# Six steps of the third modulation vector in front of the fifth SSD tile's gate projection

## The chip, the cores and the metric

One core of a Trainium2 chip runs the whole kernel in one launch. The time is the device time of that core in microseconds (us). The engines are TensorE (PE, with its weight loads as PEld), VectorE (DVE), ScalarE (ACT), GpSimd (POOL) and SyncE (SP), which here only issues loads.

## The reference, cut to what matters

Two blocks of a sequence model on 512 tokens of width 1024. The change lies in the first block, in its SSD branch and its modulation vectors:

```python
mod = jax.nn.silu(c) @ w_mod[l] + b_mod[l]              # 1024 -> 6 x 1024
sh1, sc1, gt1, sh2, sc2, gt2 = jnp.split(mod[:, None, :], N_MOD, axis=-1)
...
p_lat = h_lat @ w_in                                    # latent tokens, 512
p_ctx = h_ctx @ w_in                                    # context tokens, 256
xs_l, bm_l, cm_l, dt_l, la_l = ssd_prepare(p_lat[..., XBC0:DT0], ...)
y_l, _, _ = ssd_bidir(xs_l, bm_l, cm_l, dt_l, la_l, hf_c, hb_c, True)
ssd_lat = ssd_output(y_l, xs_l, p_lat[..., Z0:XBC0], d_skip, ssd_g)   # gated by silu(z)
...
x = x + gt1 * o_lat
x = x + gt2 * conv_ffn(modulate(x, norm2_g[l], sh2, sc2), ...)
```

`sh1` and `sc1` (vectors 0 and 1) are needed before the projections. `gt1` (vector 2) and `sh2` (vector 3) are needed after the branches, long after the SSD part.

## The kernel before, in words

**Tiles.** The SSD branch has 2048 channels, worked on as 16 tiles of 128 channels (two heads each), in four groups of four tiles. `ssd_in(kt)` does the input side of tile `kt`: at the first tile of a group the group's B and C projections (`ssd_group`), then the tile's own `xs` projection (`both`: latent and context tokens, into PSUM tiles `pl` and `pc`), convolution, transposes, chunk states (`st`), and last the gate projection z (`proj(T_Z + kt, False)`, into `pl` alone) with its silu (`zs`). `ssd_heads(kt)` does the output side: decay rows loaded by POOL (`es`, `cf`), scans and products on VectorE, and the product `y` on TensorE (line 659, raised in priority). The loop runs `ssd_in(kt + 1)` and then `ssd_heads(kt)`, and after every fourth tile `ssd_out`, the output projection of a group (`po`). In this text B1, C1 are the projections of the second group, and xs4, z4 those of `kt` = 4, the fifth tile.

**A projection.** `dense` loads a weight block of 128 x 1024 by `load_w`: one load of 512 KB on SP's queue into a tile `raw` (three of them, tag "raw"), then ScalarE makes `whi` (line 183) and VectorE `wlo` (line 186), two tiles of each. `mm3` (lines 223 to 225) issues three matmuls for each of the 8 blocks of 128 inputs: 24 matmuls into `pl`, and for `both` 24 into `pc` as well. The results lie in four PSUM banks (`bank`, tag "d") until a convolution (lines 183 and 189: `cv` for `pl`, `cvc` for `pc`) or a silu has read them.

**Modulation steps.** `mod_steps(r, ...)` computes vector `r` in 8 steps. Each step loads one block of `w_mod` (512 KB, line 341, SP's queue, the same three `raw` tiles) and issues four matmuls of 32 columns that lie beside each other in the array (line 322, `mod`, eight records of the trace a step), into a PSUM tile of its own, tag "m". After the eighth step ScalarE copies the result (`modsb`), TensorE transposes it (`modt`) and VectorE adds the bias. Vectors 0 and 1 are done before the projections, vectors 2 and 3 in the SSD loop: the list `mods` has 16 steps, and the loop takes two after each of the tiles 5 to 12.

**Order.** The program's order is not the engines' order. A planner in the compiler simulates the engines and gives each the ready instruction of highest priority; earlier in the program is higher. `tc.issue_after(ins)` puts the instructions of its block behind `ins` on the engine that `ins` runs on, and adds no wait between engines. A `raw` tile is given back when its last reader is done: `wlo` for a weight, the matmuls of the step for a modulation block.

Of the kernel before, what the change touches and what calls it, by code (L numbers as in the profile page):

```python
# [21 lines left out]
KD = 8  # L22
# [19 lines left out]
T_XBC, T_DT, T_Q, T_K, T_Z, T_G = 0, 24, 25, 33, 35, 51  # L42
# [114 lines left out]
def emit(ctx, tc, A, out):  # L157
# [22 lines left out]
    V, S, G, T, DMA, QS = nc.vector, nc.scalar, nc.gpsimd, nc.tensor, nc.sync, nc.gpsimd  # L180

    def act(o, i, f, **kw):
        return S.activation(o, i, f, **kw)  # L183

    def tt(o, a, b, op, eng=V):
        return eng.tensor_tensor(o, a, b, op=op)  # L186

    def stt(o, a, s, b, op0, op1):
        return V.scalar_tensor_tensor(o, a, s, b, op0=op0, op1=op1)  # L189
# [9 lines left out]
    def col(n, i=0, w=1):  # L199
        o = COL_OFF[n][0] + i  # L200
        return cols[:, o:o + w]
# [9 lines left out]
    def bank(name="d"):  # L211
        return banks["p"].tile([P, 512], F32, tag="d", name=name, bufs=banks["n"])
# [14 lines left out]
    def dense(src, kts, acts, outs, k0=0, kall=None):  # L227

        kall = kall or kts
        done = 0  # L230
        while done < kts:
            n = min(8, kts - done)
            hi, lo = load_w(src[:, done * P:(done + n) * P], n * P)
            for j in range(n):
                k = k0 + done + j
                for (ah, al), ps in zip(acts, outs):
                    mm3(ps, hi[:, j * P:(j + 1) * P], lo[:, j * P:(j + 1) * P],
                        ah(k), al(k), k == 0, k == kall - 1)
            done += n

    def flat(ap):
        return ap.rearrange("p k m -> p (k m)")
# [65 lines left out]
    csil = cst.tile([P, 8, 32], F32, name="csil")  # L308
# [3 lines left out]
    act(csil[:, :, 0:2], cc, AF.Silu)  # L312

    mod_end = {}

    def mod_steps(r, src, step=2, bank=bank):

        ps = bank("mod")
        for k in range(KD):
            raw = src(k)  # L320
            for j in range(4):
                T.matmul(ps[32 * j:32 * j + 32, 0:256], lhsT=csil[:, k, :], rhs=raw[:, j * 256:(j + 1) * 256],
                         start=(k == 0), stop=(k == KD - 1))
            if k % step == step - 1 and k < KD - 1:
                yield
        sb = cst.tile([P, 256], F32, tag="modsb", name="modsb")
        mod_end[r] = act(sb, ps[:, 0:256], AF.Copy).ins
        pt = bank("modt")
        for b in range(2):
            T.transpose(pt[:, b * P:(b + 1) * P], sb[:, b * P:(b + 1) * P], ident)  # L330
        v = pt[:, 0:256].rearrange("p (b j r) -> p b j r", b=2, j=4)
        bm = col("bmod", r * 8, 8).rearrange("p (j b) -> p b j", b=2)
        tt(modx[:, r, :].rearrange("p (j b) -> p b j", b=2), v[:, :, :, 0], bm, ADD)
        if r < 2:
            tt(modc[:, r, :].rearrange("p (j b) -> p b j", b=2), v[:, :, :, 1], bm, ADD)
        yield

    def mod_raw(r):
        def src(k):
            raw = wp.tile([P, 1024], F32, tag="raw", name="raw", bufs=3)  # L340
            DMA.dma_start(out=raw, in_=A["w_mod"][k * P:(k + 1) * P, r * 1024:(r + 1) * 1024])
            return raw
        return src
# [10 lines left out]
    with pool("pin") as pin, tc.tile_pool(name="pn", bufs=1, space=PSUM, reuse_waits="tile") as pn:  # L354
# [24 lines left out]
        def pnm(name):  # L379
            return pn.tile([P, 512], F32, tag="m", name=name, bufs=1)  # L380

        run(mod_steps(1, mod_pair(1), 2, pnm))
        wdt = pin.tile([P, 1024], F32, name="wdt")
        wdh = pin.tile([P, 1024], F32R, name="wdh")
# [48 lines left out]
    def proj(t, both):  # L433
        a = bank("pl")
        if both:
            c = bank("pc")
            dense(flat(A["w_ta"][t]), KD, [actl, actc], [a, c[:, 0:LC]])
            return a, c[:, 0:LC]
        dense(flat(A["w_ta"][t]), KD, [actl], [a])
        return a  # L440
# [8 lines left out]
    ps = pss.enter_context(tc.tile_pool(name="pss", bufs=1, space=PSUM, reuse_waits="tile"))  # L449

    def pst(name="t"):
        return ps.tile([P, 512], F32, tag="t", name=name, bufs=2)
# [19 lines left out]
    def silu(o, v):  # L472
        with ExitStack() as st:
            for h in hold:
                st.enter_context(tc.issue_after(h))
            act(o, v, AF.Silu)
# [74 lines left out]
    def both(t, tag, bufs, tm, tmbufs):  # L551

        a, c = proj(t, True)
        xc = sp.tile([P, LC], F32, tag="xc", name="xc")
        x = sp.tile([P, L], F32, tag=tag, name=tag, bufs=bufs)
        convs(t, [(c, LC, xc), (a, L, x)])
        xt_ = sp.tile([P, 6, P], F32, tag=tm, name=tm, bufs=tmbufs)
        to_tm([(0, [xc[:, j * P:(j + 1) * P] for j in range(2)]),
               (2, [x[:, j * P:(j + 1) * P] for j in range(4)])], xt_)
        return x, xt_  # L560
# [3 lines left out]
    def ssd_group(g):  # L564
        bl, btm = both(16 + g, "bl", 1, "btm", 2)
        t = 20 + g
        a = proj(t, False)
        cl = sp.tile([P, L], F32, tag="cl", name="cl", bufs=2)
        convs(t, [(a, L, cl)])
        cbt = sp.tile([P, L], F32, tag="cbt", name="cbt", bufs=2)  # L570
        pt = pst("cb")
        for c in range(4):
            T.matmul(pt[:, c * P:(c + 1) * P], lhsT=bl[:, c * P:(c + 1) * P], rhs=cl[:, c * P:(c + 1) * P],
                     start=True, stop=True)
        act(cbt, pt, AF.Copy)
        grp[g] = (btm, cl, cbt)
# [4 lines left out]
    def ssd_in(kt):  # L581

        g = kt // 4
        if kt % 4 == 0:
            ssd_group(g)
        btm = grp[g][0]
        xs, xtm = both(kt, "xs", 3, "xtm", 2)
        hin = []
        for d in range(2):
            xw = sp.tile([P, 6, P], F32, tag="xw", name="xw", bufs=2)  # L590
            w0 = 64 + d * 32 + 2 * kt
            for c0, c1 in ((0, 5),) if d == 0 else ((0, 2), (3, 6)):
                tt(xw[:, c0:c1].rearrange("p c (h e) -> p c h e", h=2),
                   xtm[:, c0:c1].rearrange("p c (h e) -> p c h e", h=2),
                   dwt[:, c0:c1, w0:w0 + 2].unsqueeze(3).to_broadcast([P, c1 - c0, 2, 64]), MUL,
                   eng=V)
            pst_ = pst("st")
            for n in range(4):
                cs = (0, 1) if n == 0 else (ORDER[d][n - 1],)
                for x, c in enumerate(cs):  # L600
                    T.matmul(pst_[:, n * P:(n + 1) * P], lhsT=btm[:, c], rhs=xw[:, c],
                             start=(x == 0), stop=(x == len(cs) - 1))
            hst = sp.tile([P, 4, P], F32, tag="hst", name="hst", bufs=4)
            dec = tdec[:, d * 32 + 2 * kt:d * 32 + 2 * kt + 2]
            act(hst[:, 0], pst_[:, 0:P], AF.Copy)
            for n in range(1, 4):
                for j in range(2):
                    e_ = slice(64 * j, 64 * j + 64)
                    stt(hst[:, n, e_], hst[:, n - 1, e_], dec[:, j, n:n + 1], pst_[:, n * P + 64 * j:n * P + 64 * j + 64],
                        MUL, ADD)  # L610
            hin.append(hst)
        a = proj(T_Z + kt, False)
        zs = sp.tile([P, L], F32, tag="zs", name="zs", bufs=2)
        silu(zs, a)
        pend[kt] = (xs, xtm, hin, zs)
# [73 lines left out]
    def psm(name):  # L689
        return ps.tile([P, 512], F32, tag="m", name=name, bufs=1)  # L690

    mods = [st_ for r in (2, 3) for st_ in [mod_steps(r, mod_raw(r), 1, psm)] * 8]
    with tc.issue_after(loaded.ins), tc.issue_after(mod_end[0]):
        ssd_in(0)
    hold.clear()
    early.clear()
    for kt in range(16):
        if kt < 14:
            ssd_in(kt + 1)
        ssd_heads(kt)  # L700
        if kt >= 5 and kt < 13:
            for _ in range(2):
                next(mods.pop(0))
        if kt % 4 == 1 and kt > 1:
            if kt == 13:
                ssd_in(15)
            ssd_out(kt // 4 - 1)
# [11 lines left out]
    ps = psa.enter_context(tc.tile_pool(name="psa", bufs=1, space=PSUM, reuse_waits="tile"))  # L719
# [20 lines left out]
    for i in range(2):  # L740
        a, c = proj(T_K + i, True)
# [641 lines left out]
    for kc in range(4):  # L1383
        w_h, w_l = load_w(A["w_mv"][:, 2 * kc:2 * kc + 2].rearrange("p k m -> p (k m)"))
        for k2 in range(2):
            k = 2 * kc + k2
# [17 lines left out]
    def proj2(t):  # L1404
        a = bank("p2")
        dense(flat(A["w_tb"][t]), KD, [acth], [a])
        return a
# [13 lines left out]
    ps = sta.enter_context(tc.tile_pool(name="psf", bufs=1, space=PSUM, reuse_waits="tile"))  # L1421
# [11 lines left out]
    for q in range(6):  # L1433
        a = proj2(U_U + q)
# [344 lines left out]
    for kc in range(4):  # L1779
        raw = wp.tile([P, 1024], F32, tag="raw", name="raw", bufs=3)  # L1780
# [49 lines left out]
```

## Time and profile before

| | us |
|---|---|
| median of 3 runs (2028.99 to 2034.67) | 2029.27 |
| the profiled execution | 2029.36 |
| its span, first to last instruction | 2027.6 |
| TensorE busy | 1958.2 (97%) |
| VectorE busy | 1344.9 (66%) |
| ScalarE busy | 967.5 (48%) |

The rows further down are of this profiled execution. Times in them count from the start of the span. A row of the timeline begins with the start and the length in us; a bracket at its end is the idle time of the engine before it and what ended that. TensorE's matmuls overlap, so that the spacing of their starts, not the length of one, is what a matmul costs. The granted clock (PEclk) is 1.00 at 2.4 GHz and 0.50 at 1.2 GHz.

### The profile page before, as it was taken

The numbers are of one execution on the slowest core, as the hardware profiler recorded it, in microseconds if no ns is written. First come the engines' busy times: TensorE is split into PE (matmuls) and PEld (weight loads), VectorE is DVE, ScalarE is ACT, GpSimd is POOL, SyncE is SP. The second block draws the span as 40 slices with busy tenths as digits, with TensorE's granted clock in tenths as the row PEclk, the third lists the DMA queues.
The fourth block names the chain that finished last, engine by engine and source line by source line (L and its number), as shares of the span: only waits on it lengthen the run. The fifth ranks groups of instructions, "written<-read, shape, count | busy, mean of one in ns | idle before, by whom it ended". The sixth has DMA issues, their size and how long they took to land.

```text
span 2027.6 us, 29457 instructions
## 1 busy us (share of the span) xinstructions
PE 1958.2 (97%) x11312; PEld 1612.4 (80%) x11312; DVE 1344.9 (66%) x2375; ACT 967.5 (48%) x1825; POOL 214.2 (11%) x354
## 2 busy tenths in 40 slices
PE   6998999999999899999999999999999899999998
PEld 4787888888888777778777878878988677888887
DVE  6878877879567766457988885573587655524344
ACT  6745555454246665335433244554465644423233
POOL 2111111102020000001001210000532100000000
PEclk9998999999999999999999999999999999999999
DMA  7443545545322022343354643345764121333332
GB/s 297 116 146 125 158 140 178 182 129 170 94 63 63 22 84 88 100 125 110 116 169 128 218 145 97 105 123 167 193 178 130 47 66 58 135 96 88 104 97 90
DMA packets 84667, 250.48 MB, mean 124 GB/s; under 512 B 11632, under 2 KB 23280, under 8 KB 83760
## 3 DMA queue, kind: packets, MB, share of 16 engines
q1 hardware_dynamic: 67376, 199.45, 31.9%
q0 software_dynamic: 17152, 49.17, 7.8%
q8 instruction: 89, 1.46, 0.3%
q14 instruction: 50, 0.41, 0.1%
HBM read 228.78 MB, written 16.65 MB: 121 GB/s over the span
## 4 chain that ended last, share of the span: by engine, by line
PE 89%; DVE 5%; ACT 3%; DMA 1%; issue 1%; POOL 1%; SPq 0%; DVEq 0%; ACTq 0%; POOLq 0%
PE p L223 6%; PE p L225 6%; PE p L224 6%; PE pl L223 5%; PE pl L225 5%; PE pl L224 5%; PE po L223 3%; PE po L224 3%; PE po L225 3%; PE y L659 2%; PE pT L807 2%; PE ub L225 2%; PE pdn L225 2%; PE ua L225 2%; PE pdn L223 2%; PE ub L223 2%
## 5 line engine op out<-in xcount | busy, mean ns | idle before, releaser
L186 DVE TENSOR_TENSOR wlo<-raw,whi 128x1024 fp32r<-128x1024 f32 (+3 forms) x283 | 329.1, 1164 | 275.0 <-ACT whi L183 268.6
L183 ACT ACTIVATE whi<-raw 128x1024 fp32r<-128x1024 f32 (+3 forms) x283 | 282.8, 1001 | 445.3 <-PE p L224 135.0
L223 PE MATMUL pl<-hl,whi 128*128 128x512 f32 x528 | 212.5, 403 | 10.7 <-DVE cvc L189 8.2
L225 PE MATMUL pl<-hl,wlo 128*128 128x512 f32 x528 | 210.6, 399 | 1.0 <-DVE wlo L186 1.0
L224 PE MATMUL pl<-hl,whi 128*128 128x512 f32 x528 | 210.4, 398 | 0.0
L223 PE MATMUL p<-h,whi 128*128 128x512 f32 x504 | 200.2, 399 | 1.9 <-ACT uf L183 0.8
L225 PE MATMUL p<-h,wlo 128*128 128x512 f32 x504 | 199.7, 397 | 1.1 <-DVE wlo L186 1.1
L224 PE MATMUL p<-h,whi 128*128 128x512 f32 x504 | 199.6, 396 | 0.0
L223 PEld LDWEIGHTS pl<-hl,whi 128*128 128x128 f32 x528 | 100.8, 191 | 29.0 <-issue 10.4
L225 PEld LDWEIGHTS pl<-hl,wlo 128*128 128x128 f32 x528 | 100.6, 190 | 23.6 <-DVE wlo L186 1.7
L183 ACT ACTIVATE p<-s,nm 128x512 f32<-128x512 f32 (+4 forms) x128 | 80.1, 627 | 74.0 <-PE pT L807 34.2
L223 PEld LDWEIGHTS p<-h,whi 128*128 128x128 f32 x504 | 95.3, 189 | 22.9 <-ACT uf L183 1.2
L225 PEld LDWEIGHTS p<-h,wlo 128*128 128x128 f32 x504 | 95.1, 189 | 22.2 <-DVE wlo L186 2.0
L782 DVE TENSOR_REDUCE nm<-s 128x1 f32<-128x512 f32 (+4 forms) x128 | 76.6, 610 | 53.9 <-PE s L1592 28.7
L224 PEld LDWEIGHTS pl<-hl,whi 128*128 128x128 f32 x528 | 100.7, 191 | 13.8
L224 PEld LDWEIGHTS p<-h,whi 128*128 128x128 f32 x504 | 95.1, 189 | 20.1 <-DVE h L186 0.3
L183 ACT ACTIVATE pt<-pT 128x512 f32<-128x512 f32 (+1 forms) x152 | 70.7, 478 | 64.7 <-PE pT L807 52.8
L183 ACT ACTIVATE inj<-cs_t,dwt 128x128 f32<-128x128 f32 x256 | 80.9, 393 | 34.7 <-DVE es L635 27.7
L807 PE MATMUL pT<-cs_t,p 128*128 128x128 f32 x440 | 73.5, 281 | 9.9 <-ACT pt L183 9.6
L640 POOL DMA_DIRECT2D cf<-rows x64 | 34.7, 548 | 349.0 <-PE y L659 345.0
L225 PE MATMUL ua<-hf,wlo 128*128 128x512 f32 x176 | 69.4, 394 | 0.7 <-DVE wlo L186 0.7
L225 PE MATMUL ub<-hf,wlo 128*128 128x512 f32 x176 | 70.0, 398 | 0.0
(543 smaller groups left out, 4757.5 us busy)
## 6 DMA issues: line engine op xcount, KB each, us to landing
raw<-in_w_ta SPq DMA_DIRECT2D x66, 512.0 KB, 3.6
raw<-in_w_tb SPq DMA_DIRECT2D x63, 512.0 KB, 3.6
raw<-in_w_up SPq DMA_DIRECT2D x44, 512.0 KB, 3.6
es<-rows POOLq DMA_DIRECT2D x64, 256.0 KB, 5.7
cf<-rows POOLq DMA_DIRECT2D x64, 256.0 KB, 4.9
raw<-in_w_mod SPq DMA_DIRECT2D x32, 512.0 KB, 3.8
raw<-in_w_os SPq DMA_DIRECT2D x16, 512.0 KB, 3.8
raw<-in_w_out SPq DMA_DIRECT2D x16, 512.0 KB, 3.6
```

The source lines that it names most:

```text
L183: return S.activation(o, i, f, **kw)
L186: return eng.tensor_tensor(o, a, b, op=op)
L223: T.matmul(ps, lhsT=wh, rhs=ah, start=first, stop=False)
L224: T.matmul(ps, lhsT=wh, rhs=al, start=False, stop=False)
L225: T.matmul(ps, lhsT=wl, rhs=ah, start=False, stop=last)
L640: QS.dma_start(out=c_, in_=rows[r, 1].partition_broadcast(P))
L659: mm = T.matmul(py[64 * j:64 * j + 64, sl], lhsT=lt, rhs=rh, start=(step == 2), stop=(step == 0)).ins
L782: V.tensor_reduce(nm[:, j:j + 1], src, axis=AX.X, op=MAX)
L807: T.transpose(pt[:, j * P:(j + 1) * P], b, ident)
```

## The change

`mod_steps` keeps its last matmul in `mod_mm`. In `ssd_in(4)`, between the chunk states and the gate projection z4, six of the sixteen steps are taken from `mods`, and z4's matmuls are put behind the last matmul of the sixth step. The other ten steps are taken one per tile, from `kt` = 5 to 14, where it was two per tile from 5 to 12. So the first vector of the two ends at tile 6 (before: 8), the second at tile 14 (before: 12). Nothing is computed otherwise.

```diff
     mod_end = {}
+    mod_mm = [None]
...
             for j in range(4):
-                T.matmul(ps[32 * j:32 * j + 32, 0:256], lhsT=csil[:, k, :], rhs=raw[:, j * 256:(j + 1) * 256],
-                         start=(k == 0), stop=(k == KD - 1))
+                mod_mm[0] = T.matmul(ps[32 * j:32 * j + 32, 0:256], lhsT=csil[:, k, :],
+                                     rhs=raw[:, j * 256:(j + 1) * 256], start=(k == 0), stop=(k == KD - 1)).ins
...
             hin.append(hst)
-        a = proj(T_Z + kt, False)
+        if kt == 4:
+
+            for _ in range(6):
+                next(mods.pop(0))
+        with tc.issue_after(mod_mm[0]) if kt == 4 else ExitStack():
+            a = proj(T_Z + kt, False)
...
         ssd_heads(kt)
-        if kt >= 5 and kt < 13:
-            for _ in range(2):
-                next(mods.pop(0))
+        if kt >= 5 and mods:
+            next(mods.pop(0))
```

## Rows read from the trace of the kernel before

**Rows 1.** The page: busy time by engine, and the chain that ended last.
```profile
PE 1958.2 (97%) x11312; PEld 1612.4 (80%) x11312; DVE 1344.9 (66%) x2375; ACT 967.5 (48%) x1825; POOL 214.2 (11%) x354
...
PE 89%; DVE 5%; ACT 3%; DMA 1%; issue 1%; POOL 1%; SPq 0%; DVEq 0%; ACTq 0%; POOLq 0%
```
**Rows 2.** TensorE's waits, 181.2 to 557 us: total us, times, longest.
```profile
PE pl L223 <- DVE cvc L189: 8.2, 1, 8.2
```
**Rows 3.** Timeline of TensorE around that wait: start, length, line, operation.
```profile
170.38 2.50 PE L601 MATMUL st<-xw,btm 128*128 128x128 f32 x20 [0.28 <-DVE xw L186]
181.13 0.76 PE L223 MATMUL pl<-hl,whi 128*128 128x512 f32 x1 [8.25 <-DVE cvc L189]
...
188.15 0.39 PE L223 MATMUL pl<-hl,whi 128*128 128x512 f32 x1
188.38 0.39 PE L224 MATMUL pl<-hl,whi 128*128 128x512 f32 x1
...
189.51 0.40 PE L223 MATMUL pl<-hl,whi 128*128 128x512 f32 x1
```
**Rows 4.** Matmuls into `pl` up to 181 us (lines 224, 225 alike).
```profile
L223 PE MATMUL pl<-hl,whi x104: 387/396/628, 49.2 to 162.8; 128*128 128x512 f32 x104
```
**Rows 5.** Windows: length, busy PE, PEld, DVE, ACT, POOL, clock, DMA share, GB/s.
```profile
172.90:174.00 1.10, 0.00 (x0) 0.00 (x0) 1.10 (x3) 1.10 (x3) 0.00 (x0) 1.00 1.02 380
177.00:178.00 1.00, 0.00 (x0) 0.00 (x0) 1.00 (x2) 0.64 (x2) 0.00 (x0) 0.50 0.58 234
```
**Rows 6.** The chain that ended last, 164 to 181 us: start, length, what.
```profile
164.23 2.82 PE y L659 x48
...
173.54 0.97 DVE wlo L186
...
180.60 0.39 DVE cvc L189
```
**Rows 7.** Timeline of TensorE around a pair of steps and a single step.
```profile
230.19 0.39 PE L225 MATMUL pl<-hl,wlo 128*128 128x512 f32 x1
230.51 1.07 PE L322 MATMUL mod<-raw,csil 128*32 128x256 f32 x16
231.51 0.50 PE L223 MATMUL po<-yh,whi 128*128 128x512 f32 x1
...
276.66 0.39 PE L225 MATMUL pl<-hl,wlo 128*128 128x512 f32 x1
276.98 0.64 PE L322 MATMUL mod<-raw,csil 128*32 128x256 f32 x8
277.54 0.50 PE L223 MATMUL pl<-hl,whi 128*128 128x512 f32 x1
```
**Rows 8.** The matmuls of the sixteen steps, 225 to 500 us.
```profile
L322 PE MATMUL mod<-raw,csil x128: 379/379/403, 230.5 to 454.2; 128*32 128x256 f32 x128
```
**Rows 9.** Timeline of VectorE at 161 us.
```profile
161.34 1.21 DVE L186 TENSOR_TENSOR wlo<-raw,whi 128x1024 fp32r<-128x1024 f32 x1
```
**Rows 10.** Timeline of SP: three issues of weight loads.
```profile
137.11 0.33 SPq L217 DMA_DIRECT2D raw<-in_w_ta  x1
...
156.90 0.33 SPq L217 DMA_DIRECT2D raw<-in_w_ta  x1
...
162.58 0.33 SPq L217 DMA_DIRECT2D raw<-in_w_ta  x1
```
**Rows 11.** Weight loads issued by SP from 140 to 180 us.
```profile
DMA to landing us min/median/max: 3.4/3.5/8.0
```
**Rows 12.** Timeline of TensorE between xs4's two products.
```profile
163.26 0.39 PE L225 MATMUL pl<-hl,wlo 128*128 128x512 f32 x1
...
163.63 0.37 PE L223 MATMUL pc<-hc,whi 128*128 128x256 f32 x1
```
**Rows 13.** Timeline of ScalarE: one `whi`.
```profile
158.02 1.06 ACT L183 ACTIVATE whi<-raw 128x1024 fp32r<-128x1024 f32 x1 [0.98 <-PE pl L224]
```
**Rows 14.** TensorE's timeline at 98 us, and the window from 102.
```profile
98.52 0.50 PE L223 MATMUL pl<-hl,whi 128*128 128x512 f32 x1 [1.95 <-ACT whi L183]
...
102.00:104.00 2.00, 2.00 (x8) 1.71 (x7) 2.00 (x3) 2.00 (x5) 0.00 (x0) 0.50 0.70 199
```

## What the change should do to the time

> **What bounds the kernel now.** I read the page's busy shares and the chain that ended last first [rows 1]: TensorE is busy 97% of the span and carries 89% of the chain. So the question is where TensorE stands still, and what a matmul costs where it does not. The table of who waited for whom, for TensorE from 181 us on, has one row until 557 us, and it is the wait that ends at 181.13 [rows 2]. The engine's own order of work shows it: the twenty matmuls of a chunk state (`st`) start at 170.38 and last 2.50 us, then nothing for 8.25 us, then a projection (`pl`) from 181.13 [rows 3]. Which projection? Up to there 104 matmuls of `pl` ran on each of the three lines of `mm3`, 312 in all [rows 4], at 24 per projection thirteen of them. In the order of the code those are B0 C0 xs0 z0 xs1 z1 xs2 z2 xs3 z3 B1 C1 xs4, so the one that waits is z4, the fifth tile's gate projection, in front of which the change puts the six steps.
>
> The idle stretch costs twice. The granted clock is 1.00 at its start and 0.50, the 1.2 GHz level, from 177 us on [rows 5]. z4 therefore runs from 181.13 to the first matmul behind it at 189.51, 8.4 us, where 24 matmuls at the later spacing of 0.23 us (188.15 to 188.38) would be 5.5 us [rows 3]: 2.9 us on top of the 8.25.
>
> The chain of waits says why z4 is late [rows 6]: the output product `y` of the third tile (`ssd_heads(2)`), at 164.23, releases VectorE, and VectorE then works without a pause to the second tap of the `cvc` convolution at 180.60, which gives a PSUM bank back. It is VectorE's queue behind `y`, not missing weights.
>
> **Removed from the later tiles.** Two steps together take TensorE from the last projection matmul at 230.19 to the next dense one at 231.51: 1.32 us, less the usual 0.23, is 1.09. One step alone takes 276.66 to 277.54, 0.88 less 0.23, is 0.65 [rows 7]. The sixteen steps have 128 matmul records, eight each [rows 8]; the timeline has them as five pairs and six single ones: 5 x 1.09 + 6 x 0.65 = 9.35 us. After the change ten single ones are left there: 10 x 0.65 = 6.5. **Gain 2.9 us**, all on the path, because TensorE has no wait there. Bounds: 2.9, and 3.9 with every step priced as a single one (6 x 0.65). The copy and two transposes behind each eighth step are there before and after alike and only change their tile: nothing.
>
> **Added in front of z4.** Six steps of 0.55 us (half of the pair's 1.09) are 3.3 us of TensorE. They need no bank of z4's kind (they write tile `m`), no VectorE, no ScalarE, and nothing of POOL's queue. They would fit in the 8.25 us. The added order stands within TensorE's queue: z4 behind the last step, and behind z4 the projections of tile 6 and the next `y`, for which VectorE waits. What does not fit so easily is what they bring along: six loads of 512 KB on SP's queue, into the three `raw` tiles that the weights use. The ring is seen in the trace: VectorE's `wlo` at 161.34 lasts 1.21, to 162.55, and SP issues the next load at 162.58 [rows 9, 10]. So a load is issued three weights ahead, when a `raw` tile is given back. By that count the load at 137.11 is z4's, and the split that ends at 162.55 is z4's too, 18 us before it is used. After the change the three loads up to 156.90 are of steps 1 to 3, the next three tiles are given back only by the matmuls of these steps, and z4's load is the seventh: it waits for step 4 to have run. A load takes 3.4 to 3.5 us there, at worst 8.0 [rows 11].
>
> Where do the steps go? The planner sends whatever is ready by priority. Ahead of `y` it had run out of ready work: the 24 `pl` of xs4 are all out before its first `pc` (163.26, then 163.63) [rows 12], though the code alternates them. Steps 1 to 3, whose raw tiles are in by then, are ready at that place. Two cases:
> - Steps 1 to 3 stand ahead of `y`. Then `y` is late by 3 x 0.55 = 1.6 us and VectorE's queue with it: z4 could start at 182.7 instead of 181.13. xs5's `wlo`, 0.97 us of that chain [rows 6], leaves it, because xs5's load now comes later too; z4's own takes its place unless it goes behind the `cvc`. So z4 starts at 181.8 to 182.7.
> - They stand behind `st`. Then step 1 ends at 173.4, step 4's load lands 3.5 later, step 4 takes 0.55, z4's load 3.5, ScalarE's `whi` 1.06 [rows 13]: 173.4 + 3.5 + 0.55 + 3.5 + 1.06 = 182.0.
>
> Both give about 182.2, **1.1 us later than now**. Bounds for the start: 180.2, if nothing is pushed and xs5's `wlo` is out of the way (-0.9), and 186.5, if one of the two loads takes 8.0 instead of 3.5 (+5.4). z4 stays at its 8.4 us, as the clock has no row that says it holds: see the rival.
>
> **The clock.** Does it hold when the stretch is filled with bursts? A pause of 1.95 us ends at 98.52; TensorE then works in bursts, and from 102 to 104 the granted clock is 0.50 although it is busy throughout [rows 14]. The six steps make such bursts, so I take the clock as lost here too. The Trainium skill (TensorE: Matmul & The Clock Gate, "Why this matters for your kernels") says that drops within a kernel are avoided by leaving no longer idle gap between bursts of matmuls. The steps would leave only short ones: by that rule the upper level is kept and the sum is 2.9 us better. The row at 102 speaks against it, and the sum goes by the row.
>
> **The sum.** -2.9 + 1.1 = -1.8 us. Made against the profiled execution, 2029.36 us with a span of 2027.6 (1.8 us lie around the span); the median is 2029.27, so the difference does not matter: 2029.3 - 1.8 = **2027.5**. Behind z4 no engine makes TensorE wait until 557 us [rows 2], so a shift of z4's end is passed on whole.
>
> **Rivals.**
> - *The clock is held* through the stretch. The forecast gains 2.9 more: 2024.6; with the earliest start of z4 (180.2, 2.0 us before the forecast's) 2022.6. For it: the bursts break the idle time. Against it: the low level at 102 us after a pause of 1.95 [rows 14].
> - *The change does not do what it says*: the steps are all sent ahead of `y`, where TensorE is full, and nothing fills the stretch. `y` and z4 are 3.3 us later, the later tiles 2.9 earlier: +0.4, 2029.7. For it: the three raw tiles are free early and so would be the next three if steps 1 to 3 ran in 140 to 160 us. Against it: TensorE has ready work of higher priority there.
> - *Slower: the loads hold z4 up.* z4 starts at 173.4 + a + 0.55 + b + 1.06, with a and b the times of step 4's and z4's load. The eight loads of decay rows (`es`, `cf`) that `ssd_heads(3)` issues are under way then, and the DMA share is 1.02 at 172.9 to 174 [rows 5]. With a = b = 8.0 z4 starts at 191.0, 9.9 us late: 2029.3 - 2.9 + 9.9 = 2036.3. It decides from a + b = 15.1 us on (start 9.0 late, +6.1). Against it: the share falls to 0.58 at 177 [rows 5], and the median of the loads from 140 to 180 us is 3.5 [rows 11].
>
> **How the numbers follow.** A measurement of this kernel tells about 0.3%, 6.1 us, from no change. Forecast, own range 2025.5 (2029.3 - 2.9 - 0.9) to 2031.8 (2029.3 - 2.9 + 5.4): 0.46, all within 0.3%. Clock held, 2024.6 down to 2022.6: 0.26, half of it under 2023.2. Not where it is meant to be: 0.15, within. Loads late: 0.13, slower. So faster 0.13, same 0.74, slower 0.13. The range takes in the first three, 2022.6 to 2031.8, and leaves the last out.
>
> **What would show it.** Right: TensorE's order has `mod` between 163 and 181 us; z4 starts near 182 with a wait that ends by `whi` or `cvc`; granted clock 0.50 under z4; one step per tile later on; no new wait behind z4. SP's loads of `w_mod` stand at 137 to 157. Wrong: z4 at 0.23 us spacing (clock held), `mod` all before `y`, a wait on `raw` over 9 us in front of z4, or a new wait of TensorE in tiles 6 to 15, where ten steps more spread out could leave it without ready work.

## The result, and the profile after

| | kernel before | the change |
|---|---|---|
| median, us | 2030.81 | 2043.20 |
| lowest to highest, us | 2028.99 to 2034.67 | 2042.59 to 2045.12 |
| ratio, 95% interval | | 1.0063 [1.0052, 1.0074] |
| span of the profiled execution, us | 2027.6 | 2041.4 |

The change is slower by 0.6%, twice what can be told from no change. The forecast was 2027.5, and 2031.8 at most. The two profiled spans differ by 13.8 us, the medians by 12.4, so the trace holds the loss. Line numbers moved a little: `mod` is L323 in the changed kernel, its load L342, `st` L602, `y` L665.

The page of the changed kernel, busy time by engine (as [rows 1]):

```profile
PE 1965.4 (96%) x11312; PEld 1613.3 (79%) x11312; DVE 1345.3 (66%) x2375; ACT 966.1 (47%) x1825; POOL 212.6 (10%) x354
```

The work is the same to the instruction. TensorE is busy 7.2 us longer than in [rows 1], so the other half of the 13.8 us is standing still. TensorE's waits from 181.2 to 557 us, the question of [rows 2] (total us, times, longest):

```profile
PE mod L323 <- DMA raw<-in_w_mod: 6.0, 1, 6.0
PE pl L223 <- ACT whi L183: 3.0, 3, 1.3
PE po L223 <- ACT yh L183: 2.9, 1, 2.9
PE pl L225 <- DVE wlo L186: 1.3, 1, 1.3
```

One wait has become six, and the one on `cvc` is no longer among them. The first is in front of z4, the others are new. Where they lie is seen in the timeline of TensorE of the changed kernel, which answers to [rows 3]:

```profile
156.95 1.05 PE L323 MATMUL mod<-raw,csil 128*32 128x256 f32 x10
...
158.60 0.63 PE L323 MATMUL mod<-raw,csil 128*32 128x256 f32 x6
...
170.84 1.50 PE L323 MATMUL mod<-raw,csil 128*32 128x256 f32 x24
172.27 2.50 PE L602 MATMUL st<-xw,btm 128*128 128x128 f32 x20
...
180.74 1.08 PE L323 MATMUL mod<-raw,csil 128*32 128x256 f32 x8 [5.97 <-DMA raw<-in_w_mod]
183.11 0.80 PE L223 MATMUL pl<-hl,whi 128*128 128x512 f32 x1 [1.28 <-ACT whi L183]
185.22 0.80 PE L223 MATMUL pl<-hl,whi 128*128 128x512 f32 x1 [0.89 <-ACT whi L183]
...
192.60 0.39 PE L224 MATMUL pl<-hl,whi 128*128 128x512 f32 x1
...
319.13 0.50 PE L223 MATMUL pl<-hl,whi 128*128 128x512 f32 x1 [0.80 <-ACT whi L183]
321.37 0.50 PE L225 MATMUL pl<-hl,wlo 128*128 128x512 f32 x1 [1.26 <-DVE wlo L186]
...
540.92 1.49 PE L223 MATMUL po<-yh,whi 128*128 128x512 f32 x4 [2.85 <-ACT yh L183]
...
567.16 0.50 PE L223 MATMUL pl<-hl,whi 128*128 128x512 f32 x1 [0.34 <-ACT u L183]
```

Two steps (16 records) stand ahead of the third tile's `y`, three ahead of `st`, and the sixth after a wait of 5.97 us for its own weights. Then z4 waits for its `whi`. The first two matmuls of xs5 stand among z4's in TensorE's order, and the one at 185.22 waits 0.89 us for xs5's own `whi` (ScalarE makes z4's from 182.00 on and xs5's from 184.13). The 25th matmul of `pl` from z4's first one on starts at 192.60, where it was 189.51 [rows 3]: 3.1 us late. The last line is the first matmul of the second of the two K projections that follow the SSD part; "K's projection" means this one from here on. It serves as the mark for the end of the SSD part. In the kernel before it stands here:

```profile
557.34 0.50 PE L223 MATMUL pl<-hl,whi 128*128 128x512 f32 x1 [0.34 <-ACT u L183]
```

So the SSD part as a whole ends 9.8 us late. Of 13.8 us, 9.8 are lost up to here, 6.7 of them behind z4.

**Why z4 is late** is in the loads. The instructions of SP on the line of the steps' load and on the line of the weights' load, from 171 us on (each with its count and the time from issue to landing):

```profile
L342 SPq DMA_DIRECT2D raw<-in_w_mod x1: 328/328/328, 171.5 to 171.5; - x1
DMA to landing us min/median/max: 9.2/9.2/9.2
L217 SPq DMA_DIRECT2D raw<-in_w_ta x2: 832/976/1121, 172.0 to 173.2; - x2
DMA to landing us min/median/max: 10.0/10.0/10.0
```

These are the loads of step 6, of z4 and of xs5. They leave as the `raw` tiles of steps 3 to 5 come free behind 170.84, and take 9.2 and 10.0 us, where [rows 11] had 3.5 in the middle and 8.0 at most. They are in flight with the eight loads of decay rows that POOL has issued just before. The windows show it (columns as in [rows 5]):

```profile
173.00:176.00 3.00, 1.77 (x16) 1.58 (x15) 3.00 (x6) 1.86 (x4) 0.00 (x0) 1.00 1.01 284
176.00:180.70 4.70, 0.00 (x0) 0.00 (x0) 4.70 (x10) 0.00 (x0) 0.00 (x0) 0.91 0.85 305
183.00:190.00 7.00, 6.00 (x13) 4.31 (x14) 6.91 (x14) 6.97 (x20) 0.00 (x0) 0.50 0.59 173
541.00:544.40 3.40, 3.40 (x10) 2.63 (x11) 1.59 (x3) 0.63 (x1) 0.00 (x0) 0.59 0.00 0
```

The DMA share stays at 0.85 to 1.01 from 173 to 181; [rows 5] had it at 0.58 by 177. The granted clock is 0.50, the 1.2 GHz level, under z4. And it is 0.59 for 3.4 us behind the wait at 540.92, where 10 matmuls take 3.8 us in place of 2.3.

**The sum of the 9.8 us**: z4's end 3.1 (this holds a gain of 1.2 that lies ahead of 110 us, most of it in a wait for `whi` that was 1.12 us in place of the 1.95 of [rows 14], in the same order of work as before); the waits at 319, 321 and 540 0.80 + 1.26 + 2.85 = 4.9; the low clock at 541 1.6 (e9, below, has the same wait without it); the steps in the later tiles -0.9; 1.1 are spread over the rest. From 557 to 2041 us 4.0 more are lost, and that comes at the end of the experiments.

### The profile page after: what moved, and what is told of

The parts are those of the page before. It is cut to its first block, busy times and chain, and to the rows that moved or that the text cites. A ratio compares the mean times of both kernels' runs of the same rounds, so it can differ in the third digit from the quotient of the medians.

```text
span 2041.4 us, 29463 instructions
## 1 busy us (share of the span) xinstructions
PE 1965.4 (96%) x11312; PEld 1613.3 (79%) x11312; DVE 1345.3 (66%) x2375; ACT 966.1 (47%) x1825; POOL 212.6 (10%) x354
## 5 line engine op out<-in xcount | busy, mean ns | idle before, releaser
L223 PE MATMUL pl<-hl,whi 128*128 128x512 f32 x528 | 213.2, 404 | 4.7 <-ACT whi L183 4.1
L225 PE MATMUL pl<-hl,wlo 128*128 128x512 f32 x528 | 210.4, 398 | 2.3 <-DVE wlo L186 2.3
L223 PE MATMUL p<-h,whi 128*128 128x512 f32 x504 | 200.4, 399 | 1.9 <-ACT uf L183 0.8
L225 PE MATMUL p<-h,wlo 128*128 128x512 f32 x504 | 199.9, 398 | 1.1 <-DVE wlo L186 1.1
L223 PEld LDWEIGHTS pl<-hl,whi 128*128 128x128 f32 x528 | 100.8, 191 | 24.4 <-ACT whi L183 6.6
L225 PEld LDWEIGHTS pl<-hl,wlo 128*128 128x128 f32 x528 | 100.4, 190 | 24.4 <-DVE wlo L186 3.1
L223 PEld LDWEIGHTS p<-h,whi 128*128 128x128 f32 x504 | 95.4, 189 | 22.9 <-ACT uf L183 1.2
L225 PEld LDWEIGHTS p<-h,wlo 128*128 128x128 f32 x504 | 95.2, 189 | 22.2 <-DVE wlo L186 2.0
L225 PE MATMUL ua<-hf,wlo 128*128 128x512 f32 x176 | 69.3, 394 | 1.8 <-DVE wlo L186 1.8
L225 PE MATMUL pdn<-uh,wlo 128*128 128x512 f32 x176 | 69.4, 394 | 0.8 <-DVE wlo L186 0.7
```

The lines of the kernel that those rows point to most:

```text
L223: T.matmul(ps, lhsT=wh, rhs=ah, start=first, stop=False)
L225: T.matmul(ps, lhsT=wl, rhs=ah, start=False, stop=last)
```

## The experiments

The kernels are told apart by three numbers: the ratio to the kernel before, the start of K's projection in the profile, and whether TensorE waits for `yh` of the last tile.

| kernel | ratio, 95% interval | K's projection, us | wait for `yh`, us |
|---|---|---|---|
| before | | 557.3 | none |
| the change | 1.0063 [1.0052, 1.0074] | 567.2 | 2.85 |
| e1 six in front, pairs | 1.0050 [1.0035, 1.0065] | 564.1 | 2.91 |
| e2 three in front, pairs | 1.0042 [1.0027, 1.0057] | 563.2 | 2.85 |
| e3 before, last pair split | 1.0009 [0.9998, 1.0019] | 557.6 | none |
| e4 six in front, own tile | 0.9997 [0.9987, 1.0006] | 557.6 | 2.85 |
| e5 six in front, last pairs back | 1.0022 [1.0012, 1.0032] | 561.1 | none |
| e6 own tile, last pairs back | 0.9961 [0.9947, 0.9974] | 550.5 | none |
| e7 four in front, last pairs back | 1.0030 [1.0020, 1.0040] | 558.1 | none |
| e8 before without the pair at 12 | 1.0052 [1.0034, 1.0069] | 561.4 | 2.85 |

**e1: is it the spreading?** Six in front as in the change, the other ten in pairs after tiles 5 to 9.

```diff
-        if kt >= 5 and mods:
-            next(mods.pop(0))
+        if kt >= 5:
+            for _ in range(min(2, len(mods))):
+                next(mods.pop(0))
```

> Edit: the six steps stay in front of z4, the other ten run two per tile from tile 5 to 9, so that tiles 10 to 15 have none. Theory A (two separate losses: the late loads in front of z4, about +3 to +4 us up to the next y, and the single steps spread over the late tiles, which delay y of tiles 13 to 15 and empty TensorE's queue at the end of the SSD part, about +7): the first loss stays (TensorE waits for the sixth raw tile and then for z4's whi, z4 ends 3 us late), the second is gone (no wait of TensorE between 500 and 560 us beyond the 0.3 of before); total 2031 to 2035. Rival B (the delay in front of z4 alone runs through all the tiles and is what empties the queue at the end): the wait near 540 us stays, total 2040 to 2044.

2042.2 us, by its numbers what rival B foresaw. The waits in front are the same (5.2 us on `raw`, 1.30 and 0.90 on `whi`), and the wait for `yh` stands at 539 with 2.9 us. Pairs in place of single steps don't take that wait away. So "one per tile leaves TensorE without ready work", which the prediction named as a danger, is not it.

**e2: fewer in front.** Three steps in front of z4, the other thirteen in pairs.

```diff
-            for _ in range(6):
+            for _ in range(3):
                 next(mods.pop(0))
```

> Edit: three steps in front of z4 instead of six, the other thirteen two per tile from tile 5 on. The three fit into the three raw tiles, so z4's load waits for the first step alone, which runs near 157 us, ahead of the decay-row loads at 166 to 171. Theory A (loads issued into the decay-row loads make z4 late): z4's load lands before 165, no wait for a raw tile or for z4's whi, z4 starts at 178 to 181.5; total 2025 to 2031. Rival B (any step in front of z4 costs): z4 starts after 182 and total over 2033.

2042.4 us, and z4 at 182.47 behind a wait of 7.10 us for `cvc`: by its numbers rival B. With three in front z4's load is issued at 159 us and z4 waits for no weights. It stands 14.4 us behind the last matmul of the third tile's `y`, as in the kernel before, and is late only by what stands ahead of that `y`, two of the steps; the `y` of the next tiles are 1.2 to 1.3 us late and no more. But from tile 13 on the `y` are 8 to 12 us late, and the wait for `yh` is there with 2.85 us. The front and the tail are two losses.

**e3: a later end of the steps alone.** The kernel before, with pairs after tiles 5 to 11 and single steps after 12 and 13.

```diff
-        if kt >= 5 and kt < 13:
-            for _ in range(2):
+        if kt >= 5 and mods:
+            for _ in range(2 if kt < 12 else 1):
                 next(mods.pop(0))
```

> Edit to the kernel before: only the last pair of steps (tile 12) is split into one step after tile 13 and one after tile 14; nothing in front of z4. Theory A (single steps in the last tiles delay y of tiles 13 to 15): y of tile 14 and 15 come 4 us late or more, TensorE waits near 530 us, total 2032 to 2039. Rival B (the place of these steps does not matter, the front does it all): y of tiles 13 to 15 within 1.5 us of before, total within 2 us of before.

2033.7 us, not to be told from no change. (The steps stand after tiles 12 and 13, as the edit has it, not after 13 and 14 as the expectation says.) The last three `y` are 3.7 to 5.3 us late, and TensorE does not wait: K's projection is 0.3 us later. So the output products have some slack against the end of the SSD part.

**e4: the loads in front.** The change, but the six steps load into four quarters of the tile `p1`, which is idle until the first `ssd_out`, and not into the shared `raw` tiles.

```diff
-            raw = wp.tile([P, 1024], F32, tag="raw", name="raw", bufs=3)
+            if r == 2 and k < 6:
+                raw = p1f[:, (k % 4) * 1024:(k % 4 + 1) * 1024]
+            else:
+                raw = wp.tile([P, 1024], F32, tag="raw", name="raw", bufs=3)
```

> Edit to the changed kernel: the six steps load into the four quarters of the tile p1, which is idle from the row chain (85 us) to the first ssd_out (230 us), instead of the raw tiles of the weights; everything else as changed. The loads of steps 5 and 6 wait for steps 1 and 2, those of the weights for no step. Theory A (the shared raw tiles are the cause in front of z4): z4's weights are there before 165 us as in the kernel before, TensorE has no wait for raw or whi there, z4 starts at 178 to 181.5, and the loss up to the next y (4.3 us) is gone; total 2034 to 2040 with the spread steps kept. Rival B (the steps themselves, not their loads, cost it): z4 still ends 3 us late, total as changed, 2042 to 2045.

2031.5 us, 12 us less than the change: theory A, with more gained in front than it foresaw. TensorE's timeline around z4, two windows there, and the matmuls of `pl` on one line between the third tile's `y` and z4 (the other two lines have 7 and 6 more):

```profile
174.28 1.49 PE L323 MATMUL mod<-p,csil 128*32 128x256 f32 x20
177.57 0.47 PE L223 MATMUL pl<-hl,whi 128*128 128x512 f32 x1 [1.80 <-ACT inj L183]
```

```profile
175.80:177.50 1.70, 0.00 (x0) 0.00 (x0) 1.70 (x5) 1.67 (x6) 0.00 (x0) 1.00 0.00 0
177.60:183.30 5.70, 5.70 (x25) 4.72 (x26) 5.70 (x12) 3.78 (x10) 0.00 (x0) 1.00 0.31 92
```

```profile
L224 PE MATMUL pl<-hl,whi x7: 395/396/398, 164.8 to 173.4; 128*128 128x512 f32 x7
```

No wait on weights is left in front of z4, the stretch of 8.25 us [rows 3] has shrunk to 1.80, and z4 runs at a granted clock of 1.00 in 5.6 us. Counted from the last matmul of the third tile's `y`, z4 starts 13.8 us later here, 16.5 in the change and 14.4 in the kernel before: with their own tile the steps no longer hold z4 up. But the edit did more than that. TensorE's order is another one than in the kernel before from 92 us on (in the change from 158), and `y` itself starts 3.0 us earlier than before, ahead of 20 matmuls of `pl` that stood in front of it. Those 20 and 20 records of the steps are what fills the stretch; the other 28 records ran ahead of `y`. So the late loads go away with the shared tiles, while the gain beyond that comes with the new place of `y`, and no run parted the two. The wait for `yh` stands with 2.85 us, K's projection is no earlier than before, and the gain in front is spent at the tail.

**What e5 to e8 turn on.** Behind the last `y`, TensorE has left only the `po` matmuls that were not sent ahead of it. Of the 192 of the last two groups the kernel before has 91 ahead of the last `y`, the change, e1, e2 and e4 have 132. More cannot go: the 96 of the third group, and of the fourth group nine in each of the four PSUM banks, 36; the rest needs `yh` of the last tile. e3 has 116. This number can be read from the order of the built program. So I asked whether the order of the late tiles (theory A) or the lateness handed down from the front (theory B) makes the wait.

**e5: the front of the change, the tail of before.** Single steps after tiles 5 to 10, pairs after 11 and 12; 91 again.

```diff
-        if kt >= 5 and mods:
-            next(mods.pop(0))
+        if kt >= 5:
+            for _ in range(min(2 if kt > 10 else 1, len(mods))):
+                next(mods.pop(0))
```

> The change, with its later ten steps as singles after tiles 5 to 10 and as pairs after 11 and 12 (the front part stays, loads in the three shared raw tiles). In its TensorE order 91 matmuls of po stand before the last y (as in the kernel before), in the change 132, which is all that can run without yh of tile 15. Theory A (the order of the late tiles): the front loss stays (z4 about 2 us late with its wait of about 6 us on raw), the wait of 2.85 us for yh(15) and the low clock behind it are gone, K's projection starts near 560 instead of 567.2, time 2035 to 2038. Theory B (the lateness of y out of the front is handed down by VectorE from tile to tile, whatever the order): the wait near 540 stays, 2042 to 2044.

2038.0 us, and theory A: z4 is as late as in the change (5.7 us on `raw`), its `y` are 4.1 us late at tile 3 and 3.8 to 3.9 at every tile from 12 on, and TensorE does not wait for `yh`. The `po` left behind the last `y`, by the question for the tile `po` from 527.3 us on (34 on L225 and 33 on L223 come beside these 34):

```profile
L224 PE MATMUL po<-yl,whi x34: 389/389/499, 527.4 to 550.0; 128*128 128x512 f32 x34
```

In the changed kernel the same question gives 20 on each line:

```profile
L224 PE MATMUL po<-yl,whi x20: 389/390/629, 542.2 to 555.8; 128*128 128x512 f32 x20
```

Where VectorE's time goes is seen at tile 13. VectorE in the changed kernel, whose `st` of this tile starts at 470.60, and then in e5, whose `st` starts at 469.2:

```profile
475.92 1.20 DVE L186 TENSOR_TENSOR wlo<-raw,whi 128x1024 fp32r<-128x1024 f32 x1
477.03 0.48 DVE L189 SCALAR_TENSOR_TENSOR cvc<-pc,cols,cvc 128x255 f32<-128x255 f32 x1
477.43 0.85 DVE L189 SCALAR_TENSOR_TENSOR hst<-hst,tdec,st 128x64 f32<-128x64 f32 x4
478.19 0.74 DVE L189 SCALAR_TENSOR_TENSOR cv<-pl,cols,cv 128x511 f32<-128x511 f32 x1
...
482.24 1.22 DVE L186 TENSOR_TENSOR wlo<-raw,whi 128x1024 fp32r<-128x1024 f32 x1
483.37 0.85 DVE L189 SCALAR_TENSOR_TENSOR hst<-hst,tdec,st 128x64 f32<-128x64 f32 x4
488.63 0.69 DVE L186 TENSOR_TENSOR mh<-es 128x512 f32<-128x512 f32 x1 [4.42 <-PE y L665]
```

```profile
474.17 1.60 DVE L189 SCALAR_TENSOR_TENSOR hst<-hst,tdec,st 128x64 f32<-128x64 f32 x8
475.68 0.75 DVE L189 SCALAR_TENSOR_TENSOR cv<-pl,cols,cv 128x511 f32<-128x511 f32 x1
476.34 0.66 DVE L189 SCALAR_TENSOR_TENSOR hst<-hst,tdec,st 128x64 f32<-128x64 f32 x3
...
478.05 0.26 DVE L189 SCALAR_TENSOR_TENSOR hst<-hst,tdec,st 128x64 f32<-128x64 f32 x1
```

The twelve `hst`, which `y` needs, are done 13.6 us after the start of `st` in the change and 9.1 us after it in e5. In the change the `wlo`, `cvc` and `cv` that belong to the next projections lie between them: without the pair at tile 12 TensorE has sent the next tile's projection earlier (36 matmuls of `pc` stand between the `y` of tiles 12 and 13 there, 23 in e5), and VectorE finds its results waiting. VectorE then stands still for 4.42 us until `y`. That the placing of the steps decides is shown by e5; that it acts through these instructions is read from the two traces, and no run changed them alone. The waits at 319 and 321 are not part of this: e5 has them too (0.83 and 1.28), as have e4 and e6, all with the change's single steps after tiles 5 to 10. They come right behind such a step (`mod` at 317.69), and no run took them away by itself.

**e6: both mended.** The quarters of `p1` from e4 and the placing of e5.

```diff
+            if r == 2 and k < 6:
+                raw = p1f[:, (k % 4) * 1024:(k % 4 + 1) * 1024]
...
+            for _ in range(min(2 if kt > 10 else 1, len(mods))):
```

> The same placing of the later steps, and the six steps in front load into quarters of the tile p1 instead of the raw tiles. Theory A: the gain in front of about 6 us is no longer given back at the tail; no wait for yh(15); K's projection near 552, time 2024 to 2027, faster than the kernel before. Theory B: a wait near 530 as with p1 alone, 2031 to 2033.

2023.8 us, faster than the kernel before by 0.4% [0.3, 0.5], and theory A again. z4 starts at 175.40 after a wait of 1.80 us, all the `y` from tile 12 on are 6.7 to 6.8 us earlier than before, and K's projection stands at 550.5. This version beats both kernels. Not all of its lead is made in the stretch. TensorE's order differs from 92 us on, as in e4; its waits from 92 to 117 us are 2.8 us in place of 3.8, and the granted clock is 1.00 from 102 to 106, where the kernel before has 0.50 and then 0.69 (2 us each). By these rows some 2.6 us of the lead lie there (an estimate).

**e7: four in front.** With four, z4's load is the fifth of the ring and not the seventh, and needs no other tile.

```diff
-            for _ in range(6):
+            for _ in range(4):
                 next(mods.pop(0))
...
-            next(mods.pop(0))
+            for _ in range((2, 1, 1, 1, 1, 2, 2, 2, 0, 0, 0)[kt - 5]):
+                next(mods.pop(0))
```

> Four steps in front instead of six, in the shared raw tiles; the other twelve as 2,1,1,1,1,2,2,2 after tiles 5 to 12, which leaves 91 matmuls of po before the last y. With four, z4's load is the fifth of the ring and not the seventh: it is issued at about 159 us, ahead of the decay rows' loads. If the ring's order is what hurts in front: z4's load lands by 165, no wait on raw or whi, z4 starts at 178 to 181, time 2022 to 2028. If the steps in front hurt in another way (VectorE's queue): z4 starts after 182 and the time is 2030 or more.

2038.0 us, and my theory fell. VectorE and TensorE of this kernel:

```profile
166.82 1.22 DVE L186 TENSOR_TENSOR wlo<-raw,whi 128x1024 fp32r<-128x1024 f32 x1 [4.84 <-ACT whi L183]
...
181.90 0.48 DVE L189 SCALAR_TENSOR_TENSOR cvc<-pc,cols,cvc 128x255 f32<-128x255 f32 x1
```

```profile
182.52 0.76 PE L223 MATMUL pl<-hl,whi 128*128 128x512 f32 x1 [6.44 <-DVE cvc L189]
```

z4's weights are there by 168, as foreseen. But then VectorE's queue is last again, as in the kernel before: `cvc` at 181.90, z4 at 182.5. A load in time is not enough. In e4 and e6, where z4 gained, VectorE came to the convolutions sooner, because `y` stood ahead of 20 more matmuls of `pl`; here it stands ahead of three, and starts 1.6 us later than in the kernel before. Up to K's projection e7 has lost 0.8 us; the rest of its loss lies behind 900 us, below.

**e8: only the pair at tile 12.** The kernel before, its last pair moved to one step each after tiles 10 and 11. Nothing changes in front, and 132 `po` stand ahead of the last `y`.

```diff
-        if kt >= 5 and kt < 13:
-            for _ in range(2):
+        if kt >= 5 and kt < 12:
+            for _ in range(3 if kt > 9 and kt < 12 else 2):
                 next(mods.pop(0))
```

> The kernel before, its last pair of steps moved from tile 12 to one each after tiles 10 and 11. Nothing is changed in front; 132 matmuls of po stand before the last y instead of 91. Theory A: TensorE waits 2 to 3 us for yh(15) near 525 to 540 and loses about 2 more by the clock, 2033 to 2036. Theory B: without a late y out of the front no such wait, 2029 to 2031.

Slower by 0.5%, with theory A's wait (the table of waits, and the window behind it):

```profile
PE po L223 <- ACT yh L183: 2.9, 1, 2.9
```

```profile
536.30:541.00 4.70, 4.57 (x18) 3.16 (x19) 3.66 (x6) 2.01 (x2) 0.00 (x0) 1.00 0.00 0
```

Two steps moved by one or two tiles make the tail loss with nothing changed in front. The price was larger than expected. In the profile K's projection is 4.1 us late and the span 6.9 longer; the ratio is worth 10.6. The profiled execution was the shortest of its runs, and what the longer ones lost was not seen.

**e9 and e10: the 4 us behind 900.** e9 is the change without its added order; every engine's order of instructions is the same as with it. e10 is the kernel before again.

```diff
-        with tc.issue_after(mod_mm[0]) if kt == 4 else ExitStack():
+        with ExitStack():
             a = proj(T_Z + kt, False)
```

> The change without its added order (z4 is no longer put behind the last step). Every engine's order of instructions comes out the same as in the change, so this also shows the change a second time. If the added order cost anything by itself, the time would fall; expected: none of it, 2040 to 2045. For the 4 us that the change loses behind 900 us: if the changed order there does it, the waits on wlo near 1132 and 1198 and the shift of 2.5 us between 935 and 1240 stand again; if it is the moment at which the clock falls, the 1.8 us between 903 and 935 and the low clock there may move or be gone.

> The kernel before once more, unchanged, as the counterpart: what differs between its two profiles behind 900 us is the size of what no order of instructions causes. If the fall of the clock near 915 is a matter of the moment, it may appear here (about 2 us more between 903 and 935); if the change's order causes it, it doesn't.

e9 took 2044.1 us and e10 2033.5, one execution each: with the same order of instructions as in the change, the added order costs nothing that shows. e9 also has the wait of 2.85 us for `yh`, ending at 544.30, and the granted clock behind it is 1.00, where the change had 0.59:

```profile
544.30:547.70 3.40, 3.33 (x13) 2.47 (x14) 2.35 (x5) 1.44 (x2) 0.00 (x0) 1.00 0.00 0
```

The wait near 912 us and the window behind it, in the first profile of the kernel before and then in e10:

```profile
912.57 0.50 PE L223 MATMUL po<-mgh,whi 128*128 128x512 f32 x1 [2.21 <-ACT whi L183]
```

```profile
912.50:918.00 5.50, 5.43 (x23) 4.41 (x24) 4.15 (x6) 3.04 (x7) 0.00 (x0) 1.00 0.56 182
```

```profile
912.09 0.50 PE L223 MATMUL po<-mgh,whi 128*128 128x512 f32 x1 [2.93 <-ACT whi L183]
```

```profile
912.50:918.00 5.50, 5.50 (x19) 4.36 (x18) 3.71 (x6) 2.55 (x6) 0.00 (x0) 0.69 0.46 134
```

The clock falls here in the kernel before too, in one execution and not in the other: from 903 to 935 us e10 is 2.2 us slower than the first profile of the same program, 0.7 of it by the longer wait. So the 1.8 us that the change lost there need not be its doing. Over the whole way from K's projection to the end e10 loses 3.9 us against that first profile (K's projection at 557.6, span 2031.7): as much as the change. The change's 4.0 can't be told from what two executions of one program differ by. Between 935 and 1240 us it is different: the change loses 2.5 us and e9 2.0, e10 only 0.6. There the engines' order is another one than in the kernel before (TensorE, ScalarE and VectorE between about 970 and 1230 us), in e7 too, which loses 5.1 us. TensorE's waits on `wlo` in `ua` there are 2.8 us in e7, 1.8 in the change, and 0.9 in e5, which has the order of before from 482 us to the end. e5 loses 1.2 us in this stretch and e6, with the same order, 0.5; e4, with the other order, loses 1.4. So an edit in the SSD loop has rearranged work 400 us and more behind it, and in the eight kernels with that other order the stretch is 0.8 to 4.5 us longer than in e10. That the order makes it so is argued and not shown: no run changed that order by itself, and why the planner keeps it in e5 and e6 and not in the others stays open.

## Why the prediction was wrong

**The gain in the later tiles: 2.9 forecast, 0.9 measured.** The removed part was right in its sum: the trace of before has twelve groups of `mod` where the prediction counted eleven, and priced at 9.35 they come to 9.4 us when start is subtracted from start. The ten steps that stay were priced as ten single ones of 0.65 and cost 8.5, because the planner sent five of them in two parts. The timeline of the change shows one:

```profile
279.31 0.39 PE L225 MATMUL pl<-hl,wlo 128*128 128x512 f32 x1
279.63 0.62 PE L323 MATMUL mod<-raw,csil 128*32 128x256 f32 x2
280.18 0.44 PE L549 MATMUL xT<-cs_t,xc 128*128 128x128 f32 x2
...
280.98 0.63 PE L323 MATMUL mod<-raw,csil 128*32 128x256 f32 x6
281.54 0.50 PE L223 MATMUL pl<-hl,whi 128*128 128x512 f32 x1
```

Two records take 0.55 us (279.63 to 280.18) and six take 0.56 (280.98 to 281.54); eight take 0.56 in [rows 7]. The price is one of groups, not of steps: 15 groups of 0.56 are 8.4. A pair in one group costs 1.0, so taking pairs apart loses. The Trainium skill (TensorEngine Tiling (Array Packing), "Key Properties") says that a change of the tiling mode drains the engine; the equal price of two and of eight records agrees with a cost per change of form.

**z4's start: 182.2 forecast (180.2 to 186.5), 183.1 measured.** Within the bounds, also when the 1.2 us that this execution gained ahead of 110 us are added, and the reason named, z4's load as the seventh of the ring, was the right one. But the chain was another: steps 1 and 2 went ahead of `y`, 3 to 5 ahead of `st`, and the loads of step 6 and of z4 ran side by side and not one after the other. The term that was mis-sized is the load: 3.5 us, at worst 8.0, became 9.2 and 10.0. The bound came from loads that left one by one; here three left within 2 us, into POOL's eight. That POOL's loads are issued by another engine does not help: with loads from both under way the DMA share is 1.01. The Trainium skill (DMA: Bandwidth & Descriptors, "Issuing engines are not separate DMA queues") says that transfers of all issuing engines share the same DMA engines; the row agrees. The rival "loads hold z4 up" had this mechanism. It did not come as priced, since its two loads were put in a row, and z4 was only 2 us late.

**z4's length: 8.4 forecast, 9.5 measured.** The low clock under it came as forecast (0.50 from 183 to 190). Added is the wait of 0.89 between its matmuls: two of xs5's stand among them and wait for xs5's `whi`, which no term held. Against the rival "clock held" stood a row at 102 us [rows 14]. It did not decide the question: the steps' bursts did not fill the stretch, and the clock was low behind 5.97 us that stayed empty. Where only 1.80 us stayed empty, in e4 and e6, it held at 1.00. That agrees with what the prediction cites from the Trainium skill (TensorE: Matmul & The Clock Gate, "Why this matters for your kernels") on idle gaps; [rows 14], with its pause of 1.95, still speaks the other way. The rival's price of 2.9 was right too (5.6 us in place of 8.4).

**"Behind z4 no engine makes TensorE wait, so a shift is passed on whole": this step failed, for 6.7 us.** That [rows 2] shows no wait says that the kernel before has none, not that it has room. e5 shows what the sentence meant: 4.1 us at tile 3, 3.7 at K's projection. It holds only while the order of the late tiles is the same, and the placing of the last steps, which was costed at a gain, changed it. The change's second half is what broke it: e8 makes the same wait without any step in front, e5 takes it away with all six there, and K's projection is 6.1 us earlier than in the change. I had the wait among the signs of being wrong, and gave it no price and no chance. Its reason was wrong as well: e1 has the wait with pairs, so it is not single steps as too little filler. What the traces show is a `y` that is late by VectorE's order, with too few `po` left behind the last one.

**Sum.** Forecast -2.9 + 1.1 = -1.8. In its terms the trace has -0.9 in the later tiles, +3.1 at z4's end, +4.9 + 1.6 + 1.1 behind it up to K's projection, and +4.0 after that, which two profiles of the kernel before differ by as well (3.9).

## What to carry to other kernels

A row without waits shows that an engine is fed in this order, not how much room there is. Before moving work in a planned kernel, count in the order what independent work is left behind the last product of a chain, and count it again in the changed program; a shift is passed on whole only where that order stays. And filler for an idle stretch brings its loads along: give them their own tile, so that they neither take the ring from the weights nor leave with another engine's burst.

## What the runs showed of the hardware

- A pause of the same length has both outcomes. After 2.85 us the granted clock was 0.59 from 541 us in the change, and 1.00 from 544 in e9, which runs the same order, and from 536 in e8. Near 912 us it was 1.00 behind a wait of 2.21 us in one profile of the kernel before and 0.69 behind 2.93 in the other. The fall at 541 cost some 1.6 us (10 matmuls in 3.8 us in place of 2.3, and the next ones).
- Loads of 512 KB that were issued into eight of 256 KB landed after 9.2 and 10.0 us, against 3.5 in the median and 8.0 at worst from 140 to 180 us in the kernel before [rows 11].
- Two, six or eight of the 32-column matmuls in a group cost the same 0.55 to 0.56 us; sixteen cost 1.00 [rows 7].
